# Attention scores per head on 64 rows, a fixed order of the attention's steps, and seven modulation chunks on VectorE

## The chip, the core and the metric

One core of a Trainium2 chip runs the program. TensorE (PE) multiplies, VectorE (DVE), ScalarE (ACT) and GpSimd (POOL) work elementwise, and SyncE (SP) issues nearly all DMAs. Each engine runs its own instructions in the order in which they stand in its queue; an instruction whose input or buffer isn't ready holds up all that stand behind it on that engine. The metric is the device time of the program in microseconds (us).

## The reference

256 tokens of 1024 features go through a block of two layers and then through a second, modulated block. Float32 throughout. Cut to what the change touches:

```python
# layer 0: attention with 16 query heads on 4 groups of keys, three branches with a gate each
q  = rms_norm(to_heads(x @ w_in, 16), q_gain) * 64 ** -0.5
s  = q @ k.T - slope * dist                   # selected keys, window keys, and 15 compressed keys
p  = masked_softmax(s); o = sum(gate[br] * p[br] @ v[br] for br in branches)
h  = h + o @ w_out                             # then 32 experts, then a per-layer embedding
# layer 1: the same with one branch (q normed, shared keys, no gate), experts, embedding
# second block: modulation from a vector c, then feed-forward, mixer, feed-forward
mod = silu(c) @ w_ada + b_ada                  # [1, 9 * 1024]: shift, scale, gate of each of three steps
n   = rmsnorm(h) * g * (1 + scale) + shift
h   = h + 0.5 * gate * ((silu(n @ w1_gate) * (n @ w1_up)) @ w1_down)
# the mixer: pooled half, and attention of 8 heads whose keys have a multiplicity (dilated windows)
```

With 256 tokens all four selection blocks are chosen and the windows cover all keys, so each branch is a causal attention over 256 keys.

## The kernel before

The tokens stand as two tiles of 128 rows. Each dense product is computed as three products of rounded parts (`mm3`, lines 304 to 306): a weight arrives by DMA in a buffer of the pool `raw` (nine of 1 MB), ACT writes its rounded part (line 291) and DVE what that leaves (line 292), into four buffers each of the pool `split`, and TensorE takes the parts.

The first attention (`nsa`) has **units**: a unit is one pair of heads on one branch, 16 in all (8 pairs, two branches); the second attention (`moba`) has 8 units, the mixer 4. A unit goes through `softmax_T` and `attend`:

- scores (lines 565 and 567). The keys of a group stand on a block diagonal of 128 rows: the first head's 64 features in rows 0 to 63 of one half, the second head's in rows 64 to 127 of the other, the rest zeros that GpSimd wrote (`keys`). One matmul gives both heads' scores: 256 columns for the first tile of queries, 512 for the second;
- on DVE four fused operations that add the slope and distance and take the row's extreme (line 574); on ACT four exponentials (line 579); on DVE the sum's bound, reciprocal and gate (lines 585 to 588) and the scaling of four blocks by it (line 594; `sw='svvv'` puts one of four on ACT, line 592);
- six transposes on TensorE (lines 598 to 600), copied out of PSUM by ACT (line 601, `pT`), and the products with the values (lines 608 and 610), two heads on the two halves of the columns. In `nsa` the product with the compressed values follows each pair (line 781). Then the two rounded parts of the output (lines 299 and 300).

The buffers `p` and `pT` have two of each. Nothing writes the order of these steps down: a scheduler that works through the program in its written order, with priorities (`hp`), places each instruction in its engine's queue. The queries come from two dense products of 512 columns. Behind the first, `q_norm` (squares on ACT line 493, sums line 494, Newton's steps lines 314 to 323, scaling line 512) runs and `q_T` (transposes line 347, gain lines 523 and 525) is written after the second; the second half's `q_norm`, `q_T` and compressed softmax (`compressed_softmax`, lines 697 to 715) are written behind the second pair of heads. In `moba` they stand behind the second and the fourth.

The modulation `mod` is computed in 18 **chunks** of 512 columns (`ada`), each with two weights of 1 MB, spread over the program: a chunk marked 'p' takes 16 matmuls on TensorE (line 1447) and a copy, one marked 'v' eight operations on DVE (lines 1440 and 1438). `ada_put` then needs eight small matmuls for a chunk of either kind (line 1460). `fill` says behind which step a chunk stands: chunks 2, 0, 9, 14, 1, 5 and 10 on TensorE and 3 on DVE lie in or beside the first attention, 8 and 4 in the second, 15 (TensorE), 17 and 11 (DVE) in the first feed-forward (`ffn0`).

## Time and profile before

| | us |
|---|---|
| median of three runs (1137.74 to 1517.35) | 1140.7 |
| span of the profiled execution | 1135.9 |
| TensorE busy in it | 1070.6 |
| VectorE busy | 701.9 |
| ScalarE busy | 516.2 |

The span is 4.8 us below the median. Stages in the profiled execution: first attention's scores from 84.0 and its last products at 174.1, second attention 385 to 426, first feed-forward 624 to 817. A row of the timeline has start, duration, engine, line, operation, out<-in with shapes, the count of instructions joined in the row, and in brackets the idle time before it with what ended it. A matmul's duration contains its way through the array, so the pace of TensorE is read from one start to the next.

### The profile page before, as it was taken

The numbers are of one execution on the slowest core, as the hardware profiler recorded it, in microseconds if no ns is written. First come the engines' busy times: TensorE is split into PE (matmuls) and PEld (weight loads), VectorE is DVE, ScalarE is ACT, GpSimd is POOL, SyncE is SP. The second block draws the span as 40 slices with busy tenths as digits, with TensorE's granted clock in tenths as the row PEclk, the third lists the DMA queues.
The fourth block names the chain that finished last, engine by engine and source line by source line (L and its number), as shares of the span: only waits on it lengthen the run. The fifth ranks groups of instructions, "written<-read, shape, count | busy, mean of one in ns | idle before, by whom it ended". The sixth has DMA issues, their size and how long they took to land.

```text
span 1135.9 us, 18442 instructions
## 1 busy us (share of the span) xinstructions
PE 1070.6 (94%) x7133; PEld 833.2 (73%) x7133; DVE 701.9 (62%) x1672; ACT 516.2 (45%) x995; POOL 74.3 (7%) x61
## 2 busy tenths in 40 slices
...
GB/s 375 296 185 262 277 225 304 196 372 396 416 273 170 180 336 198 286 389 323 314 350 242 168 186 213 284 173 186 224 301 175 123 185 149 174 187 159 146 22 38
DMA packets 46508, 268.57 MB, mean 236 GB/s; under 512 B 5328, under 2 KB 7120, under 8 KB 20432
## 3 DMA queue, kind: packets, MB, share of 16 engines
...
q8 instruction: 58, 0.95, 0.3%
...
## 4 chain that ended last, share of the span: by engine, by line
PE 46%; DVE 5%; ACT 1%; issue 0%; ACTq 0%; DVEq 0%
PE b L305 8%; PE b L304 8%; PE b L306 8%; PE a L304 5%; PE a L306 5%; PE a L305 5%; PE a L1054 1%; DVE nq L319 1%; DVE h L1483 1%; PE a L1094 1%; DVE rstd L323 1%; PE a L1107 1%; PE b L1460 1%; DVE w L1482 1%; PE b L1033 0%
## 5 line engine op out<-in xcount | busy, mean ns | idle before, releaser
L292 DVE TENSOR_TENSOR lo<-raw,hi 128x1024 fp32r<-128x1024 f32 (+2 forms) x220 | 256.1, 1167 | 197.7 <-ACT hi L291 195.5
L291 ACT ACTIVATE hi<-raw 128x1024 fp32r<-128x1024 f32 (+2 forms) x234 | 234.3, 1008 | 262.3 <-PE b L305 144.6
L304 PE MATMUL b<-e,hi 128*128 128x256 f32 x768 | 219.7, 286 | 2.9 <-ACT e L426 2.9
L305 PE MATMUL b<-e,hi 128*128 128x256 f32 x768 | 219.3, 285 | 0.1
L306 PE MATMUL b<-e,lo 128*128 128x256 f32 x768 | 218.9, 285 | 0.0
L304 PE MATMUL a<-hi,e 128*128 128x512 f32 (+2 forms) x512 | 199.9, 391 | 2.4 <-ACT e L364 1.8
L305 PE MATMUL a<-lo,e 128*128 128x512 f32 (+2 forms) x512 | 198.0, 387 | 0.0
L306 PE MATMUL a<-hi,e 128*128 128x512 f32 (+2 forms) x512 | 197.2, 387 | 0.5 <-DVE e L365 0.5
L304 PEld LDWEIGHTS b<-e,hi 128*128 128x128 f32 x768 | 149.2, 194 | 4.7 <-ACT e L426 3.6
L305 PEld LDWEIGHTS b<-e,hi 128*128 128x128 f32 x768 | 149.1, 194 | 1.0 <-DVE e L427 0.7
L306 PEld LDWEIGHTS b<-e,lo 128*128 128x128 f32 x768 | 149.1, 194 | 0.0
L304 PEld LDWEIGHTS a<-hi,e 128*128 128x128 f32 x512 | 96.8, 189 | 23.1 <-ACT e L364 2.9
L306 PEld LDWEIGHTS a<-hi,e 128*128 128x128 f32 x512 | 96.1, 188 | 20.7 <-DVE e L365 2.1
L305 PEld LDWEIGHTS a<-lo,e 128*128 128x128 f32 x512 | 96.9, 189 | 18.9 <-DVE lo L292 0.9
L1054 PE MATMUL a<-raw,e 128*32 128x256 f32 x832 | 73.5, 383 | 1.1 <-DVEq L1291 0.8
L579 ACT ACTIVATE p<-p,m 128x128 f32<-128x128 f32 (+1 forms) x96 | 42.6, 447 | 8.9 <-DVE m L574 6.6
L484 DVE TENSOR_TENSOR h<-h,a 128x512 f32<-128x512 f32 x48 | 32.0, 684 | 22.0 <-PE a L1107 14.7
L1054 PEld LDWEIGHTS a<-raw,e 128*32 128x32 f32 x832 | 31.4, 109 | 18.8 <-issue 2.1
L292 POOL TENSOR_TENSOR lo<-raw,hi 128x1024 fp32r<-128x1024 f32 (+1 forms) x14 | 31.4, 2267 | 205.1 <-ACT hi L291 205.0
L1097 ACT ACTIVATE w<-a,sv 128x512 fp32r<-128x512 f32 x32 | 21.6, 687 | 48.0 <-PE a L1094 47.6
L1094 PE MATMUL a<-wd,hT 128*32 128x512 f32 x256 | 43.3, 607 | 0.0
L1107 PE MATMUL a<-w,GT 128*128 128x512 f32 x128 | 36.3, 416 | 6.2 <-ACT w L1097 5.1
...
## 6 DMA issues: line engine op xcount, KB each, us to landing
...
```

The source lines that it names most:

```text
L291: nc.scalar.activation(hi[:, sl], raw[:, at], AF.Copy)
L292: eng.tensor_tensor(lo[:, sl], raw[:, at], hi[:, sl], op=OP.subtract)
L304: mm(out, l[0], r[0], start=start, stop=False, **kw)
L305: mm(out, l[0], r[1], start=False, stop=False, **kw)
L306: mm(out, l[1], r[0], start=False, stop=stop, **kw)
L319: nc.vector.scalar_tensor_tensor(q, y, h, y, op0=OP.mult, op1=OP.mult)
L484: self.nc.vector.tensor_tensor(self.h[:, t, sl], self.h[:, t, sl], ps, op=OP.add)
L579: nc.scalar.activation(p, p, AF.Exp, bias=m[:, i:i + 1], scale=-1.0, accum_out=den[:, i:i + 1])
L1054: nc.tensor.matmul(pgs[pp][32 * x:32 * x + 32], xg[:, k, o:o + 32], wg[kk][:, x], start=(k == 0), stop=(k == KT - 1))
L1094: nc.tensor.matmul(py[32 * x:32 * x + 32], hT[:, 32 * x:32 * x + 32], wd[2 * n + x // 2][:, x % 2], start=True, stop=True)
L1097: nc.scalar.activation(yh[:, sl], py, AF.Identity, scale=cw)
L1107: nc.tensor.matmul(ps, GT[:, t * P:(t + 1) * P], y[:, n * 512:(n + 1) * 512], start=(b == 0), stop=(b == len(back) - 1))
```

## The change

- `softmax_T` and `attend` are replaced by `attention`, which writes every step of every unit in a fixed order with tokens that the scheduler has to keep, on three engines: in step i the transposes and copies of unit i-2, the scores of unit i+1, the finish of unit i-3, the exponentials of unit i, the normalisation of unit i-1, the products of unit i-2, and then what `beside` puts there.
- The scores are taken per head: a matmul on rows 0 to 63 or 64 to 127 with 128 and 256 columns, four for a unit where there were two; each head's scores have a PSUM bank of their own. The keys stand on both halves of the rows without zeros, and one `raw` buffer holds two branches.
- All four blocks are scaled on DVE.
- `q_norm`, `q_T` and the compressed softmax of a half of the queries stand directly behind that half's dense product, for both halves.
- Chunks 8, 9, 10, 11, 14, 15 and 17 are computed on DVE, all inside `ffn0`; the first attention has 2, 0, 3, 1, 4 and 5 on TensorE; the second has none.

```diff
-    ada_eng='pppvpppppppvpppppv',
-    sw='svvv',
+    ada_eng='ppppppppvvvvppvvpv',
...
-    fill={'nsa:0': [2, 0], 'nsa:3': [3], 'ffn:0': [6, 7], 'mixer:0': [12, 13], 'ffn:2': [16], 'moba:3': [8, 4], 'nsa:5': [5], 'ffn0:2': [17, 15], 'nsa:2': [9, 14, 1], 'nsa:7': [10], 'ffn0:3': [11]})
+    fill={'ffn:0': [6, 7], 'ffn0:1': [8], 'ffn0:2': [9, 10], 'ffn0:3': [11, 14], 'ffn0:4': [15, 17], 'mixer:0': [12, 13],
+          'ffn:2': [16]})
 FF_GROUPS = [4, 4, 4, 4, 4, 2]
+NSA_FILL = {0: [2], 3: [0], 6: [3], 9: [1], 12: [4], 15: [5]}
+NSA_PROJECT = 7
+MOBA_PROJECT = 3
...
-    def keys(self):
-        kb = self.raw.tile([P, 4, 2, T], F32, tag="raw", name="kb")
-        for hf in range(2):
-            self.nc.gpsimd.memset(kb[64 * hf:64 * hf + 64, :, 1 - hf], 0.0)
-        return kb
+    def keys(self, n):
+        kb = self.raw.tile([P, n, 4, T], F32, tag="raw", name="kb")
+        self.KB = [kb[:, i] for i in range(n)]
 
     def put_k(self, idx, ps, gain):
-        nc = self.nc
-        for hf, eng in ((0, "s"), (1, "v")):
-            sl = slice(64 * hf, 64 * hf + 64)
-            dst = self.KB[idx // 4][sl, idx % 4:idx % 4 + 2, hf, :]
-            if gain is None:
-                self.copy(dst, ps[sl])
-            elif eng == "s":
-                nc.scalar.activation(dst, ps[sl], AF.Identity, scale=gain[sl])
-            else:
-                nc.vector.tensor_scalar(dst, ps[sl], gain[sl], None, op0=OP.mult)
...
+        dst = self.KB[idx // 4][:, idx % 4:idx % 4 + 2]
+        if gain is None:
+            self.copy(dst, ps)
+        else:
+            self.copy(dst, ps, gain)
+    def inline(self, ins):
+        self.tc.stamp_issue_order_token(ins.ins, f"attention{self.token}")
+        return ins
+    def attention(self, units, QT, slopes, dist, mult, finish, beside):
+        nc, inline = self.nc, self.inline
+        self.token += 1
+        p = [self.pp_p.tile([P, 2, 3 * P], F32, tag="p", name="p") for _ in range(2)]
+        pT = [self.pp_p.tile([P, 2, 3 * P], F32, tag="pT", name="pT") for _ in range(2)]
+        banks, dens, sums = {}, {}, {}
+        def blocks(u):
+            return [(hh, t, p[u % 2][:, hh, t * P:t * P + (t + 1) * P]) for hh in range(2) for t in range(2)]
+        def scores(u):
+            j, kb = units[u][:2]
+            banks[u] = [self.psa([P, 3 * P]) for _ in range(2)]
+            for t in range(2):
+                for hh in range(2):
+                    sl = slice(64 * hh, 64 * hh + 64)
+                    inline(nc.tensor.matmul(banks[u][hh][:, t * P:t * P + (t + 1) * P], QT[sl, j, t * P:(t + 1) * P],
+                                            kb[sl, 0:(t + 1) * P], start=True, stop=True))
+        def exponentials(u):
+            j = units[u][0]
             m = self.stat([P, 4], "m")
+            den = dens[u] = self.stat([P, 2, 2], "den")
+            s = banks.pop(u)
+            for hh, t, x in blocks(u):
+                c = 2 * t + hh
+                inline(nc.vector.tensor_tensor_reduce(
+                    out=x, in0=s[hh][:, t * P:t * P + (t + 1) * P], in1=dist[:, (1 - t) * P:2 * P],
+                    scale=-float(slopes[2 * j + hh]), scalar=3e38, op0=OP.add, op1=OP.min, accum_out=m[:, c:c + 1]))
+            for hh, t, x in blocks(u):
+                c = 2 * t + hh
                 if mult is None:
+                    inline(nc.scalar.activation(x, x, AF.Exp, bias=m[:, c:c + 1], scale=-1.0,
+                                                accum_out=den[:, t, hh:hh + 1]))
                 else:
+                    inline(nc.scalar.activation(x, x, AF.Exp, bias=m[:, c:c + 1], scale=-1.0))
+        def normal(u):
+            den = dens.pop(u)
+            if mult is not None:
+                for hh, t, x in blocks(u):
+                    inline(nc.vector.tensor_tensor_reduce(out=x, in0=x, in1=mult[:, (1 - t) * P:2 * P], scale=1.0,
+                                                          scalar=0.0, op0=OP.mult, op1=OP.add,
+                                                          accum_out=den[:, t, hh:hh + 1]))
+            w = self.stat([P, 2, 2], "w")
+            inline(nc.vector.tensor_scalar(den, den, 1e-30, None, op0=OP.max))
+            inline(nc.vector.reciprocal(w, den))
+            if units[u][3] is not None:
+                inline(nc.vector.tensor_tensor(w, w, units[u][3], op=OP.mult))
+            for hh, t, x in blocks(u):
+                inline(nc.vector.tensor_scalar(x, x, w[:, t, hh:hh + 1], None, op0=OP.mult))
+        def turn(u):
             for hh in range(2):
                 ps = self.psb([P, 3 * P])
+                for k in range(3):
+                    inline(nc.tensor.transpose(ps[:, k * P:(k + 1) * P], p[u % 2][:, hh, k * P:(k + 1) * P], self.ident))
+                inline(nc.scalar.activation(pT[u % 2][:, hh], ps, AF.Copy))
+        def products(u):
+            j, _, v, _, first, last = units[u]
+            if first:
+                sums[j] = self.psb([P, T])
+            oT, x = sums[j], pT[u % 2]
+            for hh in range(2):
+                inline(nc.tensor.matmul(oT[64 * hh:64 * hh + 64, :], v(0, hh), x[:, hh, 0:T], start=first, stop=False))
+            for hh in range(2):
+                inline(nc.tensor.matmul(oT[64 * hh:64 * hh + 64, P:T], v(1, hh), x[:, hh, T:], start=False,
+                                        stop=last is True))
+        n = len(units)
+        scores(0)
+        for i in range(n + 3):
+            if 2 <= i < n + 2:
+                turn(i - 2)
+            if i + 1 < n:
+                scores(i + 1)
+            if i >= 3 and units[i - 3][5]:
+                finish(units[i - 3][0], sums.pop(units[i - 3][0]))
+            if i < n:
+                exponentials(i)
+            if 1 <= i <= n:
+                normal(i - 1)
+            if 2 <= i < n + 2:
+                products(i - 2)
+            beside(i)
+    def put_oT(self, aT, j0, more=None):
+        def put(j, oT):
+            if more:
+                more(j, oT)
+            hi, lo = aT[0][:, j0 + j], aT[1][:, j0 + j]
+            self.inline(self.nc.scalar.activation(hi, oT, AF.Copy))
+            self.inline(self.nc.vector.tensor_tensor(lo, oT, hi, op=OP.subtract))
+        return put
...
-        def pair(j):
...
+        def compressed(j, oT):
             g = j // 2
-            oT = self.psb([P, T])
-            for br in range(2):
-                pT = self.softmax_T(j, self.KB[br][:, g], QT, self.slopes, self.c("dist"), None,
-                                    gates[:, :, 2 * j:2 * j + 2, 1 + br])
-                self.attend(oT, pT, lambda t, hh: V[:, br, t, 64 * g:64 * g + 64], br == 0, False)
             for hh in range(2):
                 o = 32 * ((2 * j + hh) % 4)
-                nc.tensor.matmul(oT[64 * hh:64 * hh + 64], self.VC[o:o + 32, g], PC[o:o + 32, g],
-                                 start=False, stop=True)
-            self.parts(aT[0][:, j], aT[1][:, j], oT)
+                self.inline(nc.tensor.matmul(oT[64 * hh:64 * hh + 64], self.VC[o:o + 32, g], PC[o:o + 32, g],
+                                             start=False, stop=True))
+        def beside(i):
+            for n in NSA_FILL.get(i, ()):
+                self.ada(n, self.psa)
+            if i == NSA_PROJECT:
+                self.project_load(0)
+                self.ada_put()
 
         self.ada_start()
         q = [self.w4([P, 2, 512]) for _ in range(2)]
         for c in range(2):
             off = self.dense(x, "w_a_in", [512], lambda ci, t, ps: self.copy(q[c][:, t], ps, r[:, t:t + 1]), off)
-            if c == 0:
-                self.q_norm(q[c])
-        self.q_T(QT, 0, q[0], qg)
-        self.compressed_softmax(0, QT, gates, PC)
+            self.q_norm(q[c])
+            self.q_T(QT, c, q[c], qg)
+            self.compressed_softmax(c, QT, gates, PC)
         aT = (self.e([P, KT, T], F32R), self.e([P, KT, T], F32R))
-        for j in range(8):
...
+        units = [(j, self.KB[br][:, j // 2], lambda t, hh, br=br, g=j // 2: V[:, br, t, 64 * g:64 * g + 64],
+                  gates[:, :, 2 * j:2 * j + 2, 1 + br], br == 0, br == 1 and "more") for j in range(8) for br in range(2)]
+        self.attention(units, QT, self.slopes, self.c("dist"), None, self.put_oT(aT, 0, compressed), beside)
+        self.ada_put()
         self.moe(0, aT, "w_a_out")
...
-            if c == 0:
-                self.q_norm(q[c])
-        self.q_T(QT, 0, q[0], qg)
+            self.q_norm(q[c])
+            self.q_T(QT, c, q[c], qg)
         aT = (self.e([P, KT, T], F32R), self.e([P, KT, T], F32R))
-        for j in range(8):
...
+        def beside(i):
+            if i == MOBA_PROJECT:
                 self.project_load(1)
+        units = [(j, self.KB[0][:, j // 2], lambda t, hh, g=j // 2: V[:, t, 64 * g:64 * g + 64], None, True, True)
+                 for j in range(8)]
+        self.attention(units, QT, self.slopes, self.c("dist"), None, self.put_oT(aT, 0), beside)
         self.moe(1, aT, "w_b_out")
...
-        for j in range(4):
...
+        units = [(j, self.KB[0][:, j], lambda t, hh, j=j: v[:, t, j * P + 64 * hh:j * P + 64 * hh + 64], None, True, True)
+                 for j in range(4)]
+        self.attention(units, QT, self.slopes2, dm[:, 0:T], dm[:, T:], self.put_oT(aT, 4), lambda i: None)
         self.dense(aT, "w_m_out", [512, 512], self.add_gated(1), tail=True)
...
-        if where in ("nsa", "moba"):
-            self.ada_put()
```

Lines of the changed kernel that the tables below name: 308 to 310 are `mm3`, 296 the split, 351 the transposes of keys and queries, 749 and 767 the compressed softmax's products and transposes, 583 the scores, 623 the transposes of the probabilities, 1487 a chunk on TensorE, 1478 and 1480 a chunk on DVE, 1564 a step of the feed-forward's activation.

TensorE inside the first half of the query projection (48 matmuls), before: the second branch's keys (`w_676`) are transposed behind 45 of them.

```order
245 L304 MATMUL a<-hi,e 128x512
246 L305 MATMUL a<-lo,e 128x512
247 L306 MATMUL a<-hi,e 128x512
248 L347 MATMUL b<-consts,w_676 128x128 x2
249 L304 MATMUL a<-hi,e 128x512
250 L305 MATMUL a<-lo,e 128x512
251 L347 MATMUL b<-consts,w_676 128x128 x6
252 L306 MATMUL a<-hi,e 128x512
```

After, the same keys (`w_669`) on the same engine:

```order
217 L309 MATMUL a<-lo,e 128x512
218 L310 MATMUL a<-hi,e 128x512
219 L308 MATMUL a<-hi,e 128x512
220 L351 MATMUL b<-consts,w_669 128x128 x2
221 L309 MATMUL a<-lo,e 128x512
222 L310 MATMUL a<-hi,e 128x512
223 L351 MATMUL b<-consts,w_669 128x128 x6
224 L308 MATMUL a<-hi,e 128x512
```

They have moved up, behind 19 of the 48.

TensorE at the end of the second half of the query projection, before; `w_705` is the first half of the queries.

```order
299 L305 MATMUL a<-lo,e 128x512
300 L306 MATMUL a<-hi,e 128x512
301 L347 MATMUL b<-consts,w_705 128x128 x8
302 L697 MATMUL a<-kc,e 128x64 x2
303 L565 MATMUL a<-kb,e 128x256
304 L697 MATMUL a<-kc,e 128x64 x6
305 L567 MATMUL a<-kb,e 128x512
306 L565 MATMUL a<-kb,e 128x256
307 L567 MATMUL a<-kb,e 128x512
```

After, at the end of the first half's product; `w_696` is the first half of the queries:

```order
249 L309 MATMUL a<-lo,e 128x512
250 L310 MATMUL a<-hi,e 128x512
251 L351 MATMUL b<-consts,w_696 128x128 x8
252 L749 MATMUL a<-kc,e 128x64 x8
253 L308 MATMUL a<-hi,e 128x512
254 L309 MATMUL a<-lo,e 128x512
```

And after, at the end of the second half's product; `w_697` is the second half:

```order
301 L310 MATMUL a<-hi,e 128x512
302 L351 MATMUL b<-consts,w_697 128x128 x8
303 L749 MATMUL a<-kc,e 128x64 x8
304 L583 MATMUL a<-kb,e 128x128 x2
305 L583 MATMUL a<-kb,e 128x256 x2
306 L583 MATMUL a<-kb,e 128x128 x2
307 L583 MATMUL a<-kb,e 128x256 x2
308 L1487 MATMUL a<-raw,c_692 32x512 x5
309 L767 MATMUL b<-consts,pc 128x128 x4
```

The transposes and the compressed scores of each half now stand directly behind that half's dense product, and the second product behind the first half's.

TensorE at the start of the second attention, before; `w_3871` is the first half of the queries.

```order
1081 L305 MATMUL a<-lo,e 128x512
1082 L306 MATMUL a<-hi,e 128x512
1083 L347 MATMUL b<-consts,w_3871 128x128 x8
1084 L565 MATMUL a<-kb,e 128x256
1085 L567 MATMUL a<-kb,e 128x512
1086 L565 MATMUL a<-kb,e 128x256
1087 L567 MATMUL a<-kb,e 128x512
1088 L565 MATMUL a<-kb,e 128x256
1089 L567 MATMUL a<-kb,e 128x512
1090 L565 MATMUL a<-kb,e 128x256
1091 L567 MATMUL a<-kb,e 128x512
1092 L598 MATMUL b<-consts,p 128x128 x2
```

After, at the same place; `w_3821` is the second half of the queries:

```order
993 L309 MATMUL a<-lo,e 128x512
994 L310 MATMUL a<-hi,e 128x512
995 L583 MATMUL a<-kb,e 128x128 x2
996 L583 MATMUL a<-kb,e 128x256 x2
997 L583 MATMUL a<-kb,e 128x128 x2
998 L583 MATMUL a<-kb,e 128x256 x2
999 L583 MATMUL a<-kb,e 128x128 x2
1000 L583 MATMUL a<-kb,e 128x256 x2
1001 L351 MATMUL b<-consts,w_3821 128x128 x8
1002 L623 MATMUL b<-consts,p 128x128 x6
```

The second half's transposes have come to stand ahead of the first transposes of probabilities.

DVE in the third group of the first feed-forward after; 7239 and 7252 are the running sums of chunks 9 and 10.

```order
1139 L296 TENSOR_TENSOR lo<-raw,hi 128x1024 x7
1140 L1564 SCALAR_TENSOR_TENSOR w_7159<-w_7159,b 128x512
1141 L1480 TENSOR_SCALAR w_7239<-raw,c_692 128x512
1142 L296 TENSOR_TENSOR lo<-raw,hi 128x1024
1143 L1564 SCALAR_TENSOR_TENSOR w_7165<-w_7165,b 128x512
1144 L1478 SCALAR_TENSOR_TENSOR w_7239<-raw,c_692,w_7239 128x512
1145 L1480 TENSOR_SCALAR w_7252<-raw,c_692 128x512
1146 L296 TENSOR_TENSOR lo<-raw,hi 128x1024
1147 L1478 SCALAR_TENSOR_TENSOR w_7239<-raw,c_692,w_7239 128x512
1148 L1478 SCALAR_TENSOR_TENSOR w_7252<-raw,c_692,w_7252 128x512
1149 L1478 SCALAR_TENSOR_TENSOR w_7239<-raw,c_692,w_7239 128x512
1150 L296 TENSOR_TENSOR lo<-raw,hi 128x1024
```

Before, the first chunk on DVE in this stage:

```order
1117 L292 TENSOR_TENSOR lo<-raw,hi 128x1024 x7
1118 L1524 SCALAR_TENSOR_TENSOR w_7229<-w_7229,b 128x512
1119 L1440 TENSOR_SCALAR w_7309<-raw,c_701 128x512
1120 L292 TENSOR_TENSOR lo<-raw,hi 128x1024
1121 L1524 SCALAR_TENSOR_TENSOR w_7235<-w_7235,b 128x512
1122 L1438 SCALAR_TENSOR_TENSOR w_7309<-raw,c_701,w_7309 128x512 x2
1123 L292 TENSOR_TENSOR lo<-raw,hi 128x1024
1124 L1438 SCALAR_TENSOR_TENSOR w_7309<-raw,c_701,w_7309 128x512 x2
```

The operations of two chunks stand between the splits of the weights, where two chunks on DVE and one on TensorE stood in the whole of this stage before.

## Rows read from the trace of the kernel before

**Rows 1.** the page of the profile: busy time of each engine.

```profile
PE 1070.6 (94%) x7133; PEld 833.2 (73%) x7133; DVE 701.9 (62%) x1672; ACT 516.2 (45%) x995; POOL 74.3 (7%) x61
```

**Rows 2.** windows: length; busy PE, PEld, DVE, ACT, POOL; granted clock; DMA share; GB/s.

```profile
84.00:170.00 86.00, 82.91 (x506) 45.62 (x506) 65.49 (x312) 57.65 (x194) 0.00 (x0) 0.98 0.65 250
385.00:426.00 41.00, 39.10 (x229) 23.22 (x226) 30.06 (x139) 32.32 (x106) 0.00 (x0) 1.00 0.73 286
624.00:817.00 193.00, 192.95 (x1367) 181.16 (x1368) 113.21 (x136) 84.18 (x99) 5.01 (x4) 0.98 0.58 207
619.70:629.90 10.20, 6.34 (x26) 5.76 (x27) 8.13 (x20) 2.75 (x7) 1.58 (x1) 0.50 0.88 371
```

**Rows 3.** TensorE in time, entry of the first attention.

```profile
69.56 0.44 PE L347 MATMUL b<-consts,w 128*128 128x128 f32 x2
...
71.20 0.39 PE L304 MATMUL a<-hi,e 128*128 128x512 f32 x1
...
82.11 1.03 PE L347 MATMUL b<-consts,w 128*128 128x128 f32 x8
...
84.00 0.65 PE L565 MATMUL a<-kb,e 128*128 128x256 f32 x2
```

**Rows 4.** DVE in time, same stretch.

```profile
68.74 1.43 DVE L535 TENSOR_TENSOR w<-w,knr 128x256 f32<-128x256 f32 x4
...
74.65 0.75 DVE L263 TENSOR_SCALAR w<-a,rstd 128x512 f32<-128x512 f32 x1
76.10 0.69 DVE L494 TENSOR_REDUCE qnv<-w 128x8 f32<-128x512 f32 x1 [0.70 <-ACT w L493]
...
79.20 1.29 DVE L512 TENSOR_TENSOR w<-w,qnr 128x512 f32<-128x512 f32 x2
```

**Rows 5.** TensorE in time, one unit of the first attention.

```profile
130.41 0.65 PE L608 MATMUL b<-pT,e 128*64 128x256 f32 x4
...
131.22 0.65 PE L781 MATMUL b<-e,vc 32*64 32x256 f32 x4
131.79 1.95 PE L1460 MATMUL b<-consts,w 128*128 128x1 f32 x16
133.60 0.31 PE L598 MATMUL b<-consts,p 128*128 128x128 f32 x1
...
133.96 0.60 PE L565 MATMUL a<-kb,e 128*128 128x256 f32 x2
134.40 1.02 PE L567 MATMUL a<-kb,e 128*128 128x512 f32 x2
135.25 0.27 PE L598 MATMUL b<-consts,p 128*128 128x128 f32 x1
```

**Rows 6.** DVE in time, same stretch.

```profile
130.26 0.81 DVE L594 TENSOR_SCALAR p<-p,w 128x128 f32<-128x128 f32 x3
130.99 0.41 DVE L574 CUSTOM_DVE_ANT_0 p<-a,consts 128x256 f32<-128x256 f32 x1
...
133.93 0.74 DVE L1438 SCALAR_TENSOR_TENSOR w<-raw,c,w 128x512 f32<-128x512 f32 x1
```

**Rows 7.** TensorE in time, last products of the first attention.

```profile
174.05 0.39 PE L610 MATMUL b<-pT,e 128*64 128x128 f32 x4
```

**Rows 8.** TensorE in time, ahead of the first feed-forward.

```profile
611.62 1.90 PE L1447 MATMUL b<-raw,c 128*32 128x512 f32 x16
...
622.06 0.48 PE L420 MATMUL a<-consts,rstd 128*128 128x128 f32 x1 [6.41 <-DVE rstd L323]
```

**Rows 9.** TensorE in time, start of the second attention.

```profile
385.08 1.04 PE L347 MATMUL b<-consts,w 128*128 128x128 f32 x8
386.35 0.67 PE L565 MATMUL a<-kb,e 128*128 128x256 f32 x2 [0.23 <-DVE e L525]
...
392.59 0.33 PE L598 MATMUL b<-consts,p 128*128 128x128 f32 x1 [0.23 <-DVE p L594]
```

**Rows 10.** TensorE in time, last products of the second attention.

```profile
425.84 0.39 PE L610 MATMUL b<-pT,e 128*64 128x128 f32 x4
```

74 lines of the change are left out of this document (4 added, 70 removed).

## Prediction

> **What bounds the kernel now.** I began with the page: TensorE is busy 94% of the span [rows 1], so I asked per stage whether it is short of work or full. In the first feed-forward it is busy 192.95 of 193 us, with DVE at 113 [rows 2]: only work taken from TensorE shortens that. The attentions look full too (82.9 of 86 us, 39.1 of 41 [rows 2]), but a matmul's duration contains its way through the array. The pace from start to start tells more. In the first attention [rows 5], three transposes take 0.36 us (133.60 to 133.96), so six take 0.7; scores 0.44 + 0.85 = 1.29; products 0.81; the compressed product 0.57 for two units; sixteen small modulation matmuls 1.81, so 0.9 a chunk. A chunk on TensorE takes 1.9 [rows 8]. Sixteen units at 0.7 + 1.29 + 0.81 + 0.29 = 3.1 are 49.5 us; six chunks 11.4, seven sets of small ones 6.3. That is 67 of the 90 us between the first scores at 84.0 [rows 3] and the last products at 174.05 [rows 7]: some 20 us are short waits of a TensorE that a step's order doesn't feed. Neither DVE (65.5) nor ACT (57.7) fills that stretch either [rows 2]. There the change can gain, at most those 20 us and what it takes away.
>
> **Entry of the first attention: a cost.** Three waits come in on TensorE, each seen in its order.
> (1) The second branch's keys are transposed behind 19 matmuls of the first query product instead of 45. Before, the transposes began at 69.56 [rows 3], as soon as DVE's scaling of the keys at 68.74 let them [rows 4]; 26 matmuls earlier at 0.23 each (82.11 less 71.20, by 48) is about 63.5. DVE has the second product's first splits behind the keys now, so it is sooner done. The wait is 0 to 5 us; I take 2.
> (2) The second product stands behind the first half's transposes and compressed scores. These wait for the queries' copy, squares, sums, Newton's steps and scaling: 74.65 to 79.20 plus 1.29, so 5.8 us [rows 4], and from the transposes to the scores 82.11 to 84.00, 1.9 [rows 3]: 7.7. Before, the second product covered all of this.
> (3) The same chain stands between the second product and the first scores: 7.7 again, where 1.9 stood. It was computed inside the attention before. Together (2) and (3) cost 15.4 - 1.9 = 13.5; between 10, if each chain is 6, and 18, if ACT's next split delays the squares.
> **The clock.** After TensorE had waited 6.41 us ahead of the feed-forward [rows 8] it was granted 0.50 for 10.2 us [rows 2], the lower of its levels. Two waits of over 7 us should do the same. The second product, 11 us at full clock, would lose 5; behind the second wait the pipeline fills and little is lost. I take 5, within 0 and 12.
> First scores: 84.0 + 2 + 13.5 + 5 = 104.5.
>
> **Steps of the attention: a gain.** Per unit DVE has four fused operations of 0.41 us and less [rows 6], some 1.2 by pace; three small ones, 0.5; four scalings, where three take 0.73 to the next operation (130.26 to 130.99 [rows 6]), so 0.95; half of a part of the output, 0.2: 2.85. There are two buffers `p`: DVE begins unit i when the transposes of i-2 have read; the scalings of i-1 stand behind that on DVE, and the transposes of i-1 wait for them. One turn of this loop is DVE's 2.85 and a hand-over, of which one costs 0.23 [rows 9]; I take 3.2. TensorE needs 3.1 a unit if the two heads' scores run one behind the other, 2.45 if side by side; either fits under 3.2, so the scores' form alone is worth nothing here. 16 x 3.2 = 51. Chunks and small matmuls in between hold TensorE: five chunks 9.5, three sets 2.7, transposes of the compressed half 0.5. Ahead of it the pipeline fills: fused operations and exponentials of unit 0, and the compressed softmax of the second half, eight operations on 256 columns (0.41 each [rows 6]) and twelve smaller ones, together about 8, under which the first chunk lies. Sum 72; last products at 176.5, so +2.4. By the order, 34 matmuls of the output's product stand ahead of the last products instead of 19: -3.4. Three sets of small matmuls follow where one did: +1.8. **First attention: +1**, from -16 (no clock loss, shorter chains, TensorE at its 60 us) to +14 (longer chains, clock lost twice, DVE held at a split of the output's weights).
>
> **Second attention: a gain.** Two chunks leave TensorE, 3.8, with 1.8 of small matmuls. Before, 385.08 to 426.2 (425.84 plus 0.39), 41.1 us [rows 9, 10], with the first transposes of probabilities 7.5 behind the start. After, they stand behind the second half's queries, whose chain of 7.7 starts at the product's end: 10.5, +3. Eight steps, without a gate, at 3.0 and 1.5 to drain give 36: -5. The output's product has ten matmuls more ahead of the end, -2.3. **-7**, between -2 and -11.
>
> **Mixer.** Multiplying by the keys' multiplicity makes DVE's step 3.9, and less product work stands between the units; before, pooling filled the same gaps. I take 0, within 3 either way: four units times less than 1 us.
>
> **First feed-forward: a small cost.** One chunk less on TensorE, -1.9; four more sets of small matmuls, +3.6: **+1.7**, fully felt, since TensorE has no idle time there. DVE takes five chunks more, each 8 operations of 0.74 [rows 6] or less, 5.7: +28.5 on 113, 74% of 193 us. They are hidden as long as the splits, which stand among them in one queue, keep ahead of the matmuls; two chunks on DVE did so before. If that cover fails, a split waits for up to two of them, 1.5 us, some five times: 0 to 8. The DMAs move 8 MB more in 193 us, 41 GB/s on 207 at a share of 0.58 [rows 2]; buffers are held longer, but it fits. GpSimd's zeros cost TensorE nothing before and give nothing back.
>
> **Sum.** +1 - 7 + 0 + 1.7 = -4.3 on the profiled 1135.9, whose median stands 4.8 above: 1140.7 - 4.3 = 1136.4; **1136**. About 2% (23 us) is what a measurement of this kernel tells from no change.
>
> **A rule weighed.** Two heads on rows 0 to 63 and 64 to 127 should overlap: no row before has two matmuls on different rows, but two heads on different columns overlap: the products take 0.81 and the scores 1.29 for the same number of columns, 4 x 256 + 4 x 128 and 2 x 256 + 2 x 512 [rows 5]. The Trainium skill, "TensorE: Matmul & The Clock Gate", Part 3, says that matmuls on different row groups run concurrently, and states 3.07 times for four tiles of 32 rows. By it the scores would take about 0.65 instead of 1.29, an estimate from that page. No run here shows it yet. The Trainium skill, "TensorEngine Tiling (Array Packing)", Tiling Modes (Key Properties), speaks against the change: a new tiling mode drains the array, and the scores are now in another mode than the transposes before them. That would give part of the gain back.
>
> **Rivals.**
> (A) *TensorE sets the step.* If the heads overlap and the fixed order feeds TensorE at 2.45 a unit, the attention is 16 x 2.45 + 13 + 8 = 60 instead of 72, the second 8 x 0.55 shorter than mine, the mixer 2; with short chains (10 instead of 13.5) and 3 off the clock: -4.3 - 12 - 4.4 - 2 - 6.5 = -29.2, 1111.5. For it: 20 us of short waits. Against: DVE's 2.85 a unit, all four scalings on it.
> (B) *Heads one behind the other.* Then TensorE's 3.1 and a hand-over of 0.23 [rows 9] at two places of a step give 3.55: 28 units x 0.35 = +10 at most, +6 with the steps that a chunk covers, so 1142.
> (C) *Slower.* The entry decides. Both chains stand open with TensorE at the low clock behind each, and DVE and ACT then meet the output's weights' splits in mid-attention, whose buffers are those of chunks 3 and 1, freed in steps 6 and 9: a late landing stops the exponentials and scalings queued behind. Chains 18, clock 12 and keys 5 are 35 instead of 20.5; a hold of 12 gives +26.5 on my sum: 1163. With these chains it is slower by over 2% from a hold of some 12 us on, and slower at all from none. For it: DMAs at 250 GB/s there; against: less to load than before.
> (D) *DVE becomes the bound of the feed-forward*: +8, 1144. Against: 74%.
>
> **How the numbers follow.** My forecast 0.45, (A) 0.25, (B) 0.13, (C) 0.10, (D) 0.07. The range takes in (A) and most of (C): 1108 to 1160. Faster by over 2%: (A) mostly and a little of mine, 0.24; slower: (C) and a little, 0.11; within 2%: 0.65.
>
> **What would show it.** Idle TensorE of 6 to 9 us twice ahead of the first scores, which begin at 101 to 109; a granted clock of 0.5 behind the first; steps of 3.0 to 3.4 us from transposes to transposes; last products of the first attention at 172 to 181; the second attention 5 to 9 us shorter; the feed-forward 193 to 197 us with TensorE full. I am wrong if the chains are hidden (scores before 95), if a step takes 2.5 (A), or if TensorE waits for splits in the feed-forward (D).

## The result, and the profile after

The changed kernel takes 1197.65 us (median of four runs, 1196.69 to 1198.94) against 1139.22 us for the kernel before: a ratio of 1.051, 95% interval 1.050 to 1.053. One of the four runs of the kernel before took 1517.35 us and stands apart from the other three (1137.61 to 1140.7). The changed kernel is slower by 5%, outside the range of the prediction. Its profiled execution has a span of 1195.3 us. The page's row of busy times answers to [rows 1]:

```profile
PE 1079.9 (90%) x7181; PEld 842.2 (70%) x7181; DVE 727.2 (61%) x1726; ACT 505.6 (42%) x961; POOL 67.3 (6%) x53
```

TensorE is busy for hardly longer (1079.9 us for 1070.6), with a net four chunks less to compute (8, 9, 10, 14 and 15 went to VectorE, 3 came back); it has a smaller part of a longer span (90% for 94%), at a mean granted clock of 0.945 for 0.977. So the question is where it stands or runs at the lower clock. The dense products are the same 3888 matmuls in both kernels (1296 sets of three), so the start of the k-th of them in each trace, subtracted, gives the lead or lag at that point of the work. The table has these differences to the trace of before, in us; the kernels of the other columns are told below.

| dense matmul (from 0), its start before | after | e1 | e2 | e5 | e6 | e8 | e10 |
|---|---|---|---|---|---|---|---|
| 95, at 35.0 (compressed keys not begun) | +0.7 | +1.1 | +1.3 | +2.0 | +1.6 | +1.1 | +0.3 |
| 96, at 42.3 (window product) | +15.3 | +1.1 | +1.3 | +2.0 | +1.6 | +1.1 | +0.3 |
| 192, at 59.1 (first query product) | +12.8 | +1.1 | +1.3 | +2.0 | +1.7 | +1.1 | +0.3 |
| 240, at 71.2 (second query product) | +25.2 | +13.6 | +1.4 | +2.2 | +1.7 | +1.1 | +0.3 |
| 288, at 169.6 (output product) | +27.5 | +14.6 | +5.1 | -0.6 | +1.0 | -6.7 | -8.2 |
| 396, at 211.4 (ahead of the first experts) | +26.2 | +13.1 | +3.6 | -5.5 | -5.2 | -9.3 | -10.8 |
| 420, at 328.2 (behind them) | +36.6 | +23.8 | +14.1 | +4.9 | -4.0 | -8.0 | -9.5 |
| 552, at 361.8 (second attention's queries) | +44.5 | +23.6 | +13.9 | +4.7 | -4.0 | -8.0 | -9.5 |
| 743, at 446.8 | +48.5 | +25.5 | +17.3 | +1.9 | -6.9 | -8.2 | -11.2 |
| 840, at 604.3 (first feed-forward) | +49.5 | +26.0 | +17.8 | +0.8 | -6.4 | -9.4 | -12.4 |
| 1993, at 787.0 (its end) | +49.0 | +25.7 | +17.1 | +0.3 | -6.9 | -10.3 | -13.1 |
| 2376, at 863.2 (mixer) | +51.4 | +28.2 | +19.3 | +2.8 | -4.3 | -8.0 | -10.6 |
| 2568, at 933.9 (mixer's end) | +58.5 | +30.4 | +21.6 | +4.7 | -3.0 | -8.0 | -10.6 |
| 3887, at 1123.8 (the last) | +58.8 | +31.4 | +22.4 | +5.8 | -1.7 | -7.8 | -10.3 |

The column of the changed kernel has six jumps: +14.6 at the compressed keys, +12.4 between the two query products, +10.4 in the first experts, +8.2 where the second attention's keys are turned (matmul 552; +36.3 one matmul earlier), about 4 more in that attention, and +7.1 in the mixer. Two of them, the first and the experts', lie in work that the diff leaves alone.

**The first jump.** TensorE of the changed kernel in time, from the compressed keys' computation to the window product:

```profile
45.90 0.44 PE L703 MATMUL b<-consts,x 128*128 128x128 f32 x2 [2.75 <-DVE x L700]
46.72 0.43 PE L717 MATMUL b<-small,w 128*128 128x64 f32 x2 [0.37 <-ACT w L709]
...
52.08 0.45 PE L734 MATMUL b<-consts,kd 128*128 128x128 f32 x1 [0.47 <-DVE nq L326]
54.82 2.12 PE L351 MATMUL b<-consts,w 128*128 128x128 f32 x8 [2.29 <-DVE w L539]
57.67 0.88 PE L308 MATMUL a<-hi,e 128*128 128x304 f32 x2 [0.73 <-ACT hi L295]
```

The same place in the trace of before (there line 651 is the changed kernel's 703, 665 its 717):

```profile
44.77 0.41 PE L651 MATMUL b<-consts,x 128*128 128x128 f32 x2
44.93 0.39 PE L305 MATMUL a<-lo,e 128*128 128x304 f32 x1
45.16 0.30 PE L306 MATMUL a<-hi,e 128*128 128x304 f32 x1
45.30 0.30 PE L304 MATMUL a<-hi,e 128*128 128x304 f32 x1
45.55 0.43 PE L665 MATMUL b<-small,w 128*128 128x64 f32 x2
```

Before, each link of the chain of small matmuls and elementwise steps stood between matmuls of the window product (128x304), and no wait shows. After, the chain stands alone, with a wait at each link, the keys' transposes (line 351) behind it, and the window product begins at 57.67. ScalarE's rows say why that product is late:

```profile
43.28 0.38 ACT L696 ACTIVATE x<-b 128x256 f32<-128x256 f32 x1 [6.68 <-PE b L693]
...
51.64 0.38 ACT L723 ACTIVATE vc<-b 128x256 f32<-128x256 f32 x1 [2.06 <-PE b L721]
56.34 0.69 ACT L265 ACTIVATE kb<-b,small 128x512 f32<-128x512 f32 x1 [4.31 <-PE b L351]
56.92 2.50 ACT L295 ACTIVATE hi<-raw 128x608 fp32r<-128x608 f32 x4
```

The product's splits (line 295) stand behind the keys' copy `kb` in ScalarE's queue. ScalarE idles 6.68, 2.06 and 4.31 us ahead of three of these rows, with the splits queued behind; before, the same four splits ran at 35.76. SyncE's transfers pause as well, in the rows of after and then of before:

```profile
22.58 21.40 SPq L278 DMA_DIRECT2D raw<-in_w_a_in  x6
59.17 5.56 SPq L278 DMA_DIRECT2D raw<-in_w_ada  x3
```

```profile
42.81 22.27 SPq L274 DMA_DIRECT2D raw<-in_w_ada  x5
```

The next weights start at 59.17 instead of 42.81.

**The chains of the queries.** Both stand open, as forecast; the rows answer to [rows 3]:

```profile
90.97 2.05 PE L351 MATMUL b<-consts,w 128*128 128x128 f32 x8 [6.76 <-DVE w L516]
92.96 3.67 PE L749 MATMUL a<-kc,e 128*128 128x64 f32 x16
...
114.89 2.12 PE L351 MATMUL b<-consts,w 128*128 128x128 f32 x8 [5.80 <-DVE w L516]
116.94 3.68 PE L749 MATMUL a<-kc,e 128*128 128x64 f32 x16
120.55 2.93 PE L583 MATMUL a<-kb,e 64*128 64x128 f32 x16
```

The first scores are at 120.55 (before 84.00 [rows 3]; forecast 104.5). Each of the three places brings a stretch at the lower clock level, 0.50, in the windows (length; busy PE, PEld, DVE, ACT, POOL; granted clock; DMA share; GB/s):

```profile
47.50:61.00 13.50, 9.97 (x39) 8.53 (x40) 9.84 (x40) 4.53 (x11) 0.00 (x0) 0.50 0.36 130
88.40:98.60 10.20, 7.63 (x29) 6.66 (x30) 6.03 (x20) 0.95 (x2) 0.00 (x0) 0.50 0.23 92
112.30:129.30 17.00, 13.46 (x57) 8.42 (x60) 10.34 (x44) 4.11 (x14) 0.00 (x0) 0.50 0.09 31
```

**The steps.** From the transposes of one unit to those of the next, with nothing between:

```profile
131.26 1.16 PE L623 MATMUL b<-consts,p 128*128 128x128 f32 x6 [0.18 <-DVE p L617]
132.35 0.93 PE L583 MATMUL a<-kb,e 64*128 64x128 f32 x8
133.20 0.65 PE L632 MATMUL b<-pT,e 128*64 128x256 f32 x4
133.69 0.39 PE L634 MATMUL b<-pT,e 128*64 128x128 f32 x4
134.00 1.06 PE L623 MATMUL b<-consts,p 128*128 128x128 f32 x6
...
143.83 1.07 PE L623 MATMUL b<-consts,p 128*128 128x128 f32 x6 [2.15 <-DVE p L617]
```

This step is 2.74 us (131.26 to 134.00), but it is the first; of the fifteen from one unit's transposes to the next, three are under 2.8 us and the median is 5.2. In the second attention, which has no chunks, they take 3.9 to 5.3. The scores take 0.85 from start to start (132.35 to 133.20), where the same number of columns took 0.44 + 0.85 = 1.29 [rows 5]. But from 120 to 208 us TensorE waits 9.5 us in four for the scaled probabilities (the last row is one of them), and DVE 14.6 us in six for ScalarE's copy of a finished output (`e`, line 660).

**The experts.** TensorE stands still at one place of the first experts, put down to its own sequencer (line 1353, the test whether an expert has too many choices). The place before, where 0.84 us of idle time are another wait, then the place after, then the window behind it:

```profile
271.92 0.62 PE L1054 MATMUL a<-raw,e 128*32 128x256 f32 x2 [0.84 <-DVEq L1291]
```

```profile
304.91 1.03 PE L1094 MATMUL a<-raw,e 128*32 128x256 f32 x2 [4.99 <-PEq L1353]
```

```profile
304.00:318.00 14.00, 13.09 (x71) 5.20 (x72) 2.42 (x9) 0.37 (x1) 1.45 (x2) 0.53 0.99 380
```

**The first feed-forward** did what was forecast; the window of 193 us from 673 answers to the third of [rows 2], with TensorE at 192.50 and DVE at 139.09:

```profile
673.00:866.00 193.00, 192.50 (x1374) 182.69 (x1375) 139.09 (x183) 83.00 (x98) 1.86 (x1) 0.98 0.69 253
```

### The profile page after: what moved, and what is told of

Its sections match the earlier page's. It is cut to its first block, busy times and chain, and to the rows that moved or that the text cites. A ratio compares the mean times of both kernels' runs of the same rounds, so it can differ in the third digit from the quotient of the medians.

```text
span 1195.3 us, 18605 instructions
## 1 busy us (share of the span) xinstructions
PE 1079.9 (90%) x7181; PEld 842.2 (70%) x7181; DVE 727.2 (61%) x1726; ACT 505.6 (42%) x961; POOL 67.3 (6%) x53
## 4 chain that ended last, share of the span: by engine, by line
PE 44%; DVE 5%; ACT 1%; issue 1%; ACTq 0%; DVEq 0%
PE b L309 8%; PE b L310 8%; PE b L308 8%; PE a L308 5%; PE a L310 5%; PE a L309 5%; PE a L1094 1%; DVE nq L323 1%; PE b L1500 1%; DVE h L1523 1%; PE a L1134 1%; PE a L1147 1%; DVE rstd L327 1%; DVE w L1522 0%; DVE lo L296 0%
## 5 line engine op out<-in xcount | busy, mean ns | idle before, releaser
L308 PE MATMUL a<-hi,e 128*128 128x512 f32 (+2 forms) x512 | 203.0, 398 | 4.5 <-ACT hi L295 1.8
L309 PE MATMUL a<-lo,e 128*128 128x512 f32 (+2 forms) x512 | 201.7, 394 | 0.0
L310 PE MATMUL a<-hi,e 128*128 128x512 f32 (+2 forms) x512 | 199.0, 391 | 0.3 <-DVE e L369 0.3
L308 PEld LDWEIGHTS a<-hi,e 128*128 128x128 f32 x512 | 98.2, 193 | 26.4 <-ACT hi L295 3.1
L310 PEld LDWEIGHTS a<-hi,e 128*128 128x128 f32 x512 | 98.1, 192 | 21.7 <-DVE e L369 1.9
L1094 PE MATMUL a<-raw,e 128*32 128x256 f32 x832 | 78.1, 396 | 5.6 <-PEq L1353 5.3
L296 POOL TENSOR_TENSOR lo<-raw,hi 128x1024 fp32r<-128x1024 f32 (+1 forms) x14 | 31.4, 2267 | 406.2 <-ACT hi L295 406.2
L599 ACT ACTIVATE p<-p,m 128x128 f32<-128x128 f32 x96 | 42.4, 444 | 9.2 <-DVE m L593 9.2
L623 PE MATMUL b<-consts,p 128*128 128x128 f32 x168 | 29.3, 303 | 15.6 <-DVE p L617 15.5
L1137 ACT ACTIVATE w<-a,sv 128x512 fp32r<-128x512 f32 x32 | 21.6, 687 | 50.1 <-PE a L1134 49.7
## 6 DMA issues: line engine op xcount, KB each, us to landing
raw<-in_w_gate SPq DMA_DIRECT2D x8, 1024.0 KB, 10.4
e<-in_moe_gu SPq DMA_DIRECT2D x6, 1024.0 KB, 10.8
```

The costliest lines, as they stand in the source:

```text
L296: eng.tensor_tensor(lo[:, sl], raw[:, at], hi[:, sl], op=OP.subtract)
L308: mm(out, l[0], r[0], start=start, stop=False, **kw)
L309: mm(out, l[0], r[1], start=False, stop=False, **kw)
L310: mm(out, l[1], r[0], start=False, stop=stop, **kw)
L599: inline(nc.scalar.activation(x, x, AF.Exp, bias=m[:, c:c + 1], scale=-1.0, accum_out=den[:, t, hh:hh + 1]))
L623: inline(nc.tensor.transpose(ps[:, k * P:(k + 1) * P], p[u % 2][:, hh, k * P:(k + 1) * P], self.ident))
```

## Experiments

Theory for the first jump and its likes (the **turn** theory): buffers of the pool `raw` are handed out in the order in which the program asks for them, and the keys' tile asks ahead of later weights. Before, GpSimd's zeros were its first writer; they wait for nothing, so the tile took its turn early and the weights behind it followed. After, its first writers are the keys' copies at the end of a chain, and the scheduler could place no later load or split until these had been placed. The built programs show it in ScalarE's queue. Before:

```
13 L261 ACTIVATE w_241<-a,rstd 128x256 x2
14 L291 ACTIVATE hi<-raw 128x608 x4
15 L644 ACTIVATE x_398<-b 128x256
```

After, the four splits have moved behind the keys' copy:

```
13 L265 ACTIVATE w_241<-a,rstd 128x256 x2
14 L696 ACTIVATE x_398<-b 128x256
15 L699 ACTIVATE x_398<-x_398 128x256
16 L709 ACTIVATE w_407<-b 128x4x16 x2
17 L726 ACTIVATE w_434,kcs<-b 128x64
18 L497 ACTIVATE w_458<-w_241 128x256
19 L497 ACTIVATE w_461<-w_241 128x256
20 L723 ACTIVATE vc<-b 128x256
21 L265 ACTIVATE kb<-b,small 128x512
22 L295 ACTIVATE hi<-raw 128x608 x4
```

Its rivals lay in the other parts of the change: the chains of the queries, the scores on 64 rows, and the fixed order itself.

### e1: the changed kernel, its keys' tile touched early

```diff
         kb = self.raw.tile([P, n, 4, T], F32, tag="raw", name="kb")
+        self.nc.gpsimd.memset(kb[:, :, :, 0:1], 0.0)
```

> The changed kernel with one thing given back: GpSimd writes one column of the keys' buffer as soon as the buffer is taken, as its zeros did before. Theory T (the buffer is handed out in turn, and without GpSimd's early write every weight behind it in the pool, and all steps that wait for those weights, are queued behind the keys): the compressed keys' chain and the keys' chains are again covered by dense products; 12 us come back ahead of the first query product, some 8 ahead of the second attention's, 4 to 6 in the mixer, in all 20 to 30, so 1168 to 1178. Rival R (the queries' chains and the half clock alone cost the 58 us): no change, 1195 to 1200.

Measured: 1169.78 us, ratio to before 1.027 (1.025 to 1.029), 27.9 us less than the changed kernel, for one small instruction whose zeros the keys overwrite. The lag at the window product falls from 15.3 to 1.1, and the jump at the second attention's keys and most of the mixer's go as well (from 28.2 to 30.4 instead of 51.4 to 58.5). SyncE's next weights start at 43.51 again:

```profile
43.51 21.76 SPq L278 DMA_DIRECT2D raw<-in_w_ada  x6
```

What follows: the turn of the tile is the largest single cause.

### e3: the kernel before, its zeros written late

The reverse test on the kernel before: GpSimd writes each zero block behind the key that stands beside it.

```diff
-        for hf in range(2):
-            self.nc.gpsimd.memset(kb[64 * hf:64 * hf + 64, :, 1 - hf], 0.0)
...
+            nc.gpsimd.tensor_scalar(self.KB[idx // 4][sl, idx % 4:idx % 4 + 2, 1 - hf, :], dst, 0.0, None, op0=OP.mult)
```

> The kernel before with the zeros of the keys' buffer written by GpSimd behind each key, from the key times 0, instead of at once; nothing else. Theory T: the same 20 to 27 us as in the changed kernel are lost here, 1159 to 1168, with TensorE waiting in the compressed keys at 45 us. Rival R: GpSimd is off the path, within 4 us of 1139.

Measured: 1177.61 us, ratio 1.034 (1.032 to 1.036). The kernel before gets the changed kernel's first and fourth jumps: +15.5 at the window product (matmul 95 +1.8, matmul 96 +17.3) and +9.0 at the second attention's keys (18.3 to 27.3); and 4.9 more behind the second attention (30.8 to 35.7, matmuls 743 and 744), which the changed kernel doesn't have. On TensorE the chain has the changed kernel's waits, 2.29 us at the transposes in both:

```profile
53.41 0.45 PE L681 MATMUL b<-consts,kd 128*128 128x128 f32 x1 [0.48 <-DVE nq L322]
56.15 2.12 PE L347 MATMUL b<-consts,w 128*128 128x128 f32 x8 [2.29 <-DVE w L535]
```

It cost more than I had expected of the turn theory. Part of that may be GpSimd's own work behind each key, which a memset ahead of them doesn't bring; that was not separated. What follows: neither the fixed order nor the 64 rows is needed for these jumps.

### e2: e1 with the second half's query steps back inside the attention

```diff
-            self.q_norm(q[c])
-            self.q_T(QT, c, q[c], qg)
-            self.compressed_softmax(c, QT, gates, PC)
+            if c == 0:
+                self.q_norm(q[c])
+        self.q_T(QT, 0, q[0], qg)
+        self.compressed_softmax(0, QT, gates, PC)
...
+            if i == 1:
+                self.q_norm(q[1])
+            if i == 3:
+                self.q_T(QT, 1, q[1], qg)
+                self.compressed_softmax(1, QT, gates, PC)
```

The same in the second attention, at steps 0 and 2.

> The changed kernel with the early write, and with the second half's query norm, transposes and compressed softmax back beside the attention's steps 1 and 3 (0 and 2 in the second attention), the first half's behind the second product. Theory T: a further 15 to 25 us come back (two chains of 6 us, the half clock behind each), 1143 to 1160; with the scores on 64 rows and the fixed order as such a gain, it goes below the kernel before, 1115 to 1139. If fixed order and scores are themselves the loss: it stays over 1165.

Measured: 1160.74 us, ratio 1.020 (1.018 to 1.022), 9.0 less than e1. The lag at the second query product is 1.4 instead of 13.6, and the first scores of a unit are at 85.48. Of these 12.2 us 2.7 are lost in the attention again: the lag at the output product falls from 14.6 to 5.1, by 9.5. TensorE's and DVE's largest waits in it (from 100 to 185 us) are these:

```profile
PE b L624 <- DVE p L618: 11.8, 4, 6.1
```

```profile
DVE e L662 <- ACT e L661: 17.1, 6, 4.3
```

I had expected 1143 to 1160, and below the kernel before if the rest of the change were a gain: what held the attention was another thing.

### e5: e2 with the finish of a unit later in the order

The finish of a unit is its compressed product on TensorE, ScalarE's copy of the sum and DVE's remainder of it.

```diff
             if i + 1 < n:
                 scores(i + 1)
-            if i >= 3 and units[i - 3][5]:
-                finish(units[i - 3][0], sums.pop(units[i - 3][0]))
             if i < n:
                 exponentials(i)
             if 1 <= i <= n:
                 normal(i - 1)
+            if i >= 3 and units[i - 3][5]:
+                finish(units[i - 3][0], sums.pop(units[i - 3][0]))
```

> This is e2_both with one thing more: in the fixed order the finish of unit i-3 on VectorE (the remainder of the per-head product's copy and the work behind it) stands behind the step that normalises unit i-1, and no longer ahead of the two fused operations of unit i. Theory F (the early finish closes a loop: VectorE waits for ScalarE's copy of a product that TensorE makes only after the turn that waits for VectorE's fused operation): the waits of the finish for ScalarE, 17.1 us in 6 in e2_both's trace, and TensorE's wait for the normalised scores, 14.2 us in 5, shrink to under half, the first attention gets 5 to 12 us shorter, the second 0 to 5, and the whole is 1143 to 1155. Rival G (TensorE waits for the normalised scores since VectorE and ScalarE split the output weights in the middle of the attention and the finish only happens to stand there): the same two waits move to other lines, the time stays within 4 us of e2_both, 1157 to 1164. The stop of TensorE of 4 to 5 us at the overflow check in the first experts is expected to stay in either case.

Measured: 1147.3 us (1143.73 to 1147.7), ratio 1.007 (1.005 to 1.008), 13.4 less than e2. Both waits fall, in the window 100 to 171:

```profile
PE b L624 <- DVE p L618: 4.3, 3, 1.7
```

```profile
DVE e L662 <- ACT e L661: 3.1, 5, 1.0
```

By the table it is 5.7 us ahead of e2 at the output product, 9.1 at matmul 396, and gains 6.2 more from matmul 552 to 743, in the second attention, where a step falls from 4.3 us to 3.1 (medians). What follows: theory F. DVE stood at the remainder of unit i-3's output, waiting for ScalarE's copy of a sum that TensorE completes only behind the transposes of unit i-2 and the scores of unit i+1, while the fused operations of unit i, which need none of this, were queued behind it. The edit moves ScalarE's copy behind its exponentials as well; the two were not separated. The trace of e5 is of an execution 3.6 us under its median, so its column in the table is low by that.

### e4: the kernel before with the scores on 64 rows alone

```diff
-            s0 = self.psa([P, 2, P])
-            nc.tensor.matmul(s0, QT[:, j, 0:P], kb[:, :, 0:P], start=True, stop=True)
-            s1 = self.psa([P, 2, T])
-            nc.tensor.matmul(s1, QT[:, j, P:T], kb, start=True, stop=True)
+            sb = [self.psa([P, 3 * P]) for _ in range(2)]
+            for t in range(2):
+                for hh in range(2):
+                    sl = slice(64 * hh, 64 * hh + 64)
+                    nc.tensor.matmul(sb[hh][:, t * P:t * P + (t + 1) * P], QT[sl, j, t * P:(t + 1) * P],
+                                     kb[sl, hh, 0:(t + 1) * P], start=True, stop=True)
```

> The kernel before with the scores per head on 64 rows alone (a PSUM bank for each head; zeros, order and chunks as before). If the two heads run side by side, a unit's scores take 0.65 to 0.9 us instead of 1.29: 28 units, 11 to 18 us less of TensorE, of which the short waits keep part: 1125 to 1137. If the scores' form is worth nothing because DVE sets the step: 1137 to 1141.

Measured: 1160.17 us, ratio 1.019 (1.017 to 1.021): slower, and both expectations missed. The lag is +0.7 ahead of the first attention, +9.3 behind it, +11.0 ahead of the first experts and +19.1 behind them. In the attention waits of TensorE grow or appear: for the block of probabilities that ScalarE scales, and for a bank that DVE has still to read. The third row is the experts (the rows are sums over the whole run):

```profile
PE b L600 <- ACT p L594: 5.3, 3, 3.2
PE a L1449 <- DVE m L576: 5.1, 2, 2.7
...
PE a L1056 <- PEq L1315: 4.9, 2, 4.6
```

So scores on 64 rows bought nothing in this order, they lost 8.6 us in the attention, and there was a second effect, in the experts, that no theory had. All kernels so far with scores on 64 rows had it; e6, e7 and e9 are on it.

### e6: e5 with the scores on 128 rows

```diff
-            banks[u] = [self.psa([P, 3 * P]) for _ in range(2)]
+            banks[u] = [self.psa([P, 2, P]), self.psa([P, 2, T])]
             for t in range(2):
-                for hh in range(2):
-                    sl = slice(64 * hh, 64 * hh + 64)
-                    inline(nc.tensor.matmul(banks[u][hh][:, t * P:t * P + (t + 1) * P], QT[sl, j, t * P:(t + 1) * P],
-                                            kb[sl, 0:(t + 1) * P], start=True, stop=True))
+                inline(nc.tensor.matmul(banks[u][t], QT[:, j, t * P:(t + 1) * P], kb[:, :, 0:(t + 1) * P],
+                                        start=True, stop=True))
```

`keys` and `put_k` are those of the kernel before, with GpSimd's zeros.

> This is e5_finish_late with the scores as in the kernel before: both heads of a pair in one matmul of 128 rows against keys that stand on a diagonal with GpSimd's zeros beside them, two banks of PSUM a unit; the fixed order of the steps on three engines stays. Theory S (the scores on 64 rows take TensorE less time in the attention, and that time is on the path): slower than e5 by 0.35 us a unit with two time blocks, 6 to 10 us over both attentions. Theory B (the form of the scores is worth nothing, since the step of a unit is set by the loop through VectorE and ScalarE, and the 64 rows only cost bank turns): within 3 us of e5 in the attention. In both the branch in the first experts is a question of its own: with the stop of 4 to 5 us and the half clock behind it gone as in the kernel before, 8 to 10 us faster than without it, which would put the whole at 1132 to 1145.

Measured: 1136.05 us, ratio 0.998 (0.997 to 0.999). Ahead of the first experts e5 and e6 stand within 0.3 us of each other (-5.5 and -5.2), and over the second attention (552 to 743) both gain 2.8 to 2.9 on before, at steps of 3.1 and 3.0 us (medians). What follows: theory B, the form of the scores is worth nothing in this loop. Behind the experts they are 8.9 apart (+4.9 and -4.0): that is the stop. The medians are 11.2 apart and the ends of the two traces 7.5; nearly all of the difference is the 3.6 by which e5's trace lies under its median.

### e7 and e9: idle matmuls ahead of the experts

e7 is the kernel before with this, and e9 is e8 (below) with 16 instead of 24:

```diff
+        pad = self.psb([P, T])
+        for _ in range(24):
+            nc.tensor.matmul(pad[:, 0:1], self.ident, self.c("ones"), start=True, stop=True)
         self.moe(0, aT, "w_a_out")
```

> This is the kernel before with 24 matmuls of one column more on TensorE, put behind the attention and ahead of the first experts, whose result nobody reads; they add work and change nothing else. Theory P (TensorE's stop of 4 to 5 us at the overflow check comes from how many instructions stand in its program before the check, not from the scores or the order): the check's branch takes over 4 us as in the changed kernel, a half clock follows, and the time is 8 to 13 us above before. Rival Q (the stop has another cause): the branch stays at 0.2 us and the time is 1 to 4 us above before.

> This is e8_chunks with 16 of the one-column matmuls of e7_pad in the same place; nobody reads their result. Ahead of the overflow check TensorE's program then holds 3439 records of matmuls and weight loads in the trace, against 3445 in the kernel before and 3443 in e3 (branch 0.21 us there) and 3509 to 3564 in the kernels that stop for 4 to 5 us. Theory P (how many instructions stand ahead of the check decides): the branch stays near 0.2 us, no half clock follows it, and the time is 1135 to 1144, the pad's own cost alone. Rival Q (matmuls like these ahead of the check stop TensorE there, however many instructions stand before): the branch takes over 4 us, the half clock follows, 1145 to 1153.

Measured: e7 1159.0 us, ratio 1.016 (1.014 to 1.018); e9 1136.48 us, 0.998 (0.997 to 1.000), 4.8 above e8. At 19.1 us above before e7 is outside both expectations, since the pad itself cost more than I had thought: its 24 matmuls (two passes each, 48 in the trace) took 8.31 us, for the granted clock fell to 0.5 for 13.65 us from 2 us into them, and the lag ahead of the experts was 11.1. Across them it grew to 19.3, and the stop was there; the second row is the window behind it:

```profile
287.03 1.03 PE L1057 MATMUL a<-raw,e 128*32 128x256 f32 x2 [4.73 <-PEq L1316]
```

```profile
286.50:300.50 14.00, 13.47 (x70) 5.28 (x71) 2.41 (x9) 0.37 (x1) 1.46 (x2) 0.51 0.99 391
```

In e9 it was not, and in the same 14 us TensorE did 113 matmuls instead of 70:

```profile
269.30 0.62 PE L1057 MATMUL a<-raw,e 128*32 128x256 f32 x2 [0.84 <-DVEq L1294]
```

```profile
269.00:283.00 14.00, 13.53 (x113) 8.00 (x117) 4.76 (x15) 2.88 (x8) 1.46 (x2) 1.00 1.01 409
```

The kernels sort themselves by how many records the trace has on TensorE up to this test: matmuls, weight loads, and its sequencer's waits and branches. (The expectation of e9 calls them matmuls and weight loads; of those alone there are 3316 to 3380 in the kernels without a stop and 3444 to 3508 in the others.)

| kernel | records | stop |
|---|---|---|
| e8, e10 | 3375 | none |
| e6 | 3383 | none |
| e9 | 3439 | none |
| e3 | 3443 | none |
| before | 3445 | none |
| e5 | 3509 | 4.9 us |
| e2 | 3511 | 4.6 us |
| after | 3513 | 5.0 us |
| e1 | 3516 | 5.3 us |
| e7 | 3541 | 4.7 us |
| e4 | 3564 | 4.6 us |

What follows: theory P, over these counts. The kernel before was 64 records or fewer from a stop that it never showed.

The traces also show what comes in at the stop. A DMA queue that the profile names `q8 instruction` moves 58 packets of 16 KB in the kernel before, one for about 250 of TensorE's records, so I take them for TensorE's program. In the six kernels without a stop one of them starts 4.5 to 5.6 us ahead of the branch. In the six others the last one started 10.5 to 13.8 us ahead, the next starts 1.6 to 2.5 us behind the branch's start and takes 0.9 to 1.1, and TensorE's next matmul starts 1.4 to 1.7 us after it. In e2 and e5 the branch itself has its usual 0.22 us, and the idle time stands behind it. So TensorE seems to wait for the code that the branch leads to; no run moved the code at an equal number of instructions, and larger numbers were not tried, so whether more instructions would always bring the stop is not shown.

### e8: the kernel before with the new places of the modulation chunks alone

```diff
-    ada_eng='pppvpppppppvpppppv',
+    ada_eng='ppppppppvvvvppvvpv',
...
-    fill={'nsa:0': [2, 0], 'nsa:3': [3], 'ffn:0': [6, 7], 'mixer:0': [12, 13], 'ffn:2': [16], 'moba:3': [8, 4], 'nsa:5': [5], 'ffn0:2': [17, 15], 'nsa:2': [9, 14, 1], 'nsa:7': [10], 'ffn0:3': [11]})
+    fill={'nsa:0': [2, 0], 'nsa:3': [3], 'ffn:0': [6, 7], 'ffn0:1': [8], 'ffn0:2': [9, 10], 'ffn0:3': [11, 14], 'ffn0:4': [15, 17], 'mixer:0': [12, 13], 'ffn:2': [16], 'nsa:5': [5], 'nsa:2': [4, 1]})
```

> This is the kernel before with the change's distribution of the modulation chunks alone: the seven chunks go to VectorE (five of them in the stretch of the first experts' feed-forward layers), the others to TensorE in the places that the change gives them. Theory C (they leave TensorE at places where VectorE has room): 2 to 6 us faster, 1134 to 1138. Rival D (VectorE becomes the bound in the first experts, or the chunks on TensorE that are left give no time back): 1139 to 1144.

Measured: 1131.7 us, ratio 0.993 (0.991 to 0.995), a gain of 8.2, more than either expectation. By the table nearly all of it is in the first attention (+1.1 to -6.7), which now has six chunks, all on TensorE, where it had seven and one on DVE. 0.9 is in the feed-forward, and 0.2 in the second attention, which two chunks left; the stages between gain or lose up to 2.6, which nearly cancel.

### e10: e8 with the fixed order in the second attention alone

The `attention` of e6 is called in `moba`; the first attention and the mixer stay with the scheduler's order.

```diff
-        for j in range(8):
-            g = j // 2
-            oT = self.psb([P, T])
-            pT = self.softmax_T(j, self.KB[0][:, g], QT, self.slopes, self.c("dist"), None, None)
...
+        units = [(j, self.KB[0][:, j // 2], lambda t, hh, g=j // 2: V[:, t, 64 * g:64 * g + 64], None, True, True)
+                 for j in range(8)]
+        self.attention(units, QT, self.slopes, self.c("dist"), None, self.put_oT(aT, 0), beside)
```

> This is e8_chunks (the scheduler's order in the first attention, zeros of GpSimd, scores on 128 rows, the change's distribution of the modulation chunks) with the fixed order of e6_128_rows in the second attention alone. Theory H (the fixed order costs in the first attention, where a unit's step carries a compressed product, gates and chunks, and gains in the second, where e6 stands 4.5 us better behind it than in front of it): 1125 to 1130. Rival I (what e6 won in the second attention came from work that the first attention had left, and the order itself is worth nothing): 1130 to 1135.

Measured: 1127.66 us, ratio 0.990 (0.989 to 0.992), the fastest of all, 4.0 below e8. By the two traces, 2.5 apart at their ends, 1.5 of these lie in the second attention (552 to 743: -1.7, in e8 -0.2) and another 1.5 ahead of the output product, whose code is the same in both (0.8 of it stands at matmul 95 already). So the number is theory H's, but how much of it the order in the second attention gives is not settled. e6, which has the order in the first attention and the mixer too, is 8.4 slower, with 5.6 of it in the lag at matmul 396; but it also has other places of the chunks inside the first attention and all four scalings on DVE there, so that the order alone costs this is not shown.

## Why the prediction was wrong

Read from the changed kernel back, the medians give the price of each part in this order of undoing: the late turn of the keys' tile 27.9 us (after less e1), the chains of the queries 9.0 (e1 less e2), the early finish 13.4 (e2 less e5), the scores on 64 rows 11.2 (e5 less e6; 8.9 of it are the stop in the experts by the traces), what is left of the fixed order 4.4 (e6 less e8; with it the fourth scaling on DVE, which no run tested alone, and the chunks' places inside the attention), and against these the chunks, which gain 8.2 (e8 against before). In another order of undoing the shares could differ.

**The step that failed first** is the sentence "GpSimd's zeros cost TensorE nothing before and give nothing back". They cost nothing, but they held the place of the keys' tile in the order of the buffers. The diff showed that they go; I asked only what TensorE, DVE and ACT would save. The order of the built program showed the result: I had read TensorE's queue at the queries, not ScalarE's at the compressed keys.

**Entry.** For the keys (1) I took 2 us. The wait that I meant cost 0.3 at most (its transposes begin at 76.51, half a microsecond behind the matmul ahead of them, at a pace of 0.23), and 12.8 came from the compressed keys ahead of it. For the two chains and the clock I took 13.5 + 5; from 12.8 to the scores' 36.6 (120.55 less 84.0) are 23.8. The waits themselves, 6.76 and 5.80, are near the 5.8 that I read from [rows 4]. Too small was what stands behind them. The transposes and compressed scores, which I had at 1.9, take 5.7 behind the second wait (114.89 to 120.55): the 1.9 of [rows 3] holds only two of a half's eight compressed products, and in e2, where all eight and the transposes run at the full clock, they take 3.5. The rest is the clock. I charged 5 us, for the stretch behind the first chain; behind the two chains 27.2 us at 0.50 came (10.2 and 17.0), and 13.5 at the keys.

**Steps.** I took 3.2 us a step; the first is 2.74, between mine and rival A's 2.45, but the median in the first attention is 5.2, and it lasted 86.2 from the first scores to the last products (120.55 to 206.7), not 72. My loop had DVE's own work, and the finish only as 0.2 us of it. Where it stands in the order was the point: e5 shows that the wait there cost the kernel 13.4. With it late, the steps of the second attention have a median of 3.1, for my 3.0: the loop was sized right and lacked this wait. Rival C, which I gave 0.10, named DVE held in mid-attention, and put it down to the splits of the output weights; its 1163 was the nearest of my cases. Its low clock behind both chains came, and the hold is shown, but the hold's cause was another.

**The scores' form.** "Worth nothing here" was right for the path (e5 and e6 ahead of the experts), and so was the reason, a step that DVE's loop sets (3.1 and 3.0 us in the second attention), though the heads overlap: 0.85 for 1.29 us, 1.5 times. The Trainium skill, "TensorE: Matmul & The Clock Gate", Part 3, says that tiles on different row groups run concurrently; this trace agrees, with a smaller factor than the 3.07 that it states for four tiles of 32 rows. How much of the rest is the drain at a new mode, of which "TensorEngine Tiling (Array Packing)", Tiling Modes, speaks, no run here separates.

**The first experts** were not in the sum at all. I had taken a stage that the diff doesn't touch to keep its length; it got 10.4 us longer, about 9 of it by the stop (1.2 to 1.3 also come in e6, e8 and e10, which have none).

**Second attention.** I took -7; it was +12.2 (36.3 to 48.5): 8.2 by the turn of the tile and 4.0 behind it. There the steps take 4.3 us (median) for my 3.0, by the early finish: with the turn mended the lag still grows by 1.9 (e1), with the chain taken out as well by 3.4 (e2), and with the finish late the stage gains 2.8 (e5). A cost of the chain alone is not shown here.

**Mixer.** I took 0; it was +7.1, of which about 5 go with e1.

**First feed-forward.** I took +1.7 and DVE at 141; it was -0.5 at 139. The cover held, and rival D is refuted. The chunks' gain lies in the first attention, 7.8 in e8, for six chunks on TensorE instead of seven and one on DVE; my sum had only TensorE's time for them. Why it is that much is not shown.

**The range** had its upper end from rival C with a hold of 12. It had no case for a cost in work that the diff leaves alone, and the first jump and the experts' are 25 of the 58.8 us.
